# A two-layer hybrid encoder on one core: modulation as products and sums on VectorE, paced by TensorE's time

## The chip, the cores and the metric

The kernel runs on one core of a Trainium2 chip. Its time is the device time of one execution in microseconds (us); three runs of the kernel before gave 2958.4, 2958.51 and 2960.57 us, median 2958.51. The execution that the profiler recorded took 2961.13 us, of which 2959.30 us is the span from the first to the last recorded instruction. In this text a slot is one 128x1024 piece of streamed weights (512 KB), the unit in which the whole program is written; a tile of the modulation has the same size.

## The reference

Two layers, 256 tokens, width 2048, all in f32. Each layer turns the conditioning vector c into six vectors of 2048 (shift, scale and gate for two sub-layers), and then runs a token mixer and a gated convolutional MLP, both behind an RMS norm that scale and shift modulate:

```python
c_act = silu(c)                                   # (1, 2048)
for l in range(2):
    mod = c_act @ w_ada[l] + b_ada[l]             # (1, 6 * 2048)
    sh1, sc1, g1, sh2, sc2, g2 = split(mod, 6)
    h = rms_norm(x, g_norm1[l]) * (1 + sc1) + sh1
    x = x + g1 * hybrid_mixer(h, ...)             # attention, S5, pooling, three gates
    h = rms_norm(x, g_norm2[l]) * (1 + sc2) + sh2
    x = x + g2 * conv_ffn(h, ...)
```

The modulation is a product of a vector with a 2048 x 12288 matrix in each layer: 192 tiles of 512 KB a layer, 384 in all. The parts are numbered 0 to 5 in the order of the split. The S5 part of the mixer is a scan over time whose output y goes through a small projection (w_glu) and then through p_b into the merge of the branches.

## The kernel before, in words

All weights are streamed in 936 slots, 468 a layer. For every slot SyncE's queue fetches 512 KB (raw, four buffers), ScalarE rounds it to fp32r (whi, `make_hi`, four buffers), VectorE subtracts to get the rest (wlo, `make_lo`, three buffers), and TensorE multiplies: for each of the eight 128x128 blocks one pass of the high part with 512 columns (the high and low halves of the activation side by side) and one of the low part with 256 columns. `block_emitter` writes all eight high passes of a slot first (line 326), then all eight low ones (line 331). The low part of slot s+2 is written ahead of the products of slot s.

A layer's slots are, in this order and counted from the layer's first: the input projections (0 to 47), the gates and branch projections (48 to 177), w_out (178 to 209), and the MLP: up, down, up, down (210 to 467). `w_glu` stands at 160 and 161, behind twelve gate blocks.

Everything else is written by generators ("tasks") that `run_stream` steps once a slot. A task may run only while a credit is positive; every VectorE instruction takes its modelled time from the credit, and every slot gives 2.6 us. What a consumer needs at once is forced by `require`, whatever the credit. So the order of the instructions on each engine is fixed when the program is built, and a consumer that comes too early puts all of its producer's remaining instructions into the queues in one piece. The engines then run their queues in order, held by semaphores alone.

The modulation is a task of low rank, in groups of tiles (`ADA`), paced by a table of slot against tile (`ADA_PLAN`). 192 of its 384 tiles go to TensorE: c is spread over 32 columns and four 32-column strips of the array work side by side, two tiles and four products at a time. The other 192 go to VectorE, as two `scalar_tensor_tensor` of 128x512 each that accumulate into `acc`; eight tiles make one `acc`, which TensorE transposes in four pieces and VectorE reduces to four columns of `mod`. The norm of a sub-layer (`norm`, `hrhs`) turns x into the operand h two blocks at a time on VectorE and ScalarE, as soon as their entries of `mod` are there, and looks ahead by four blocks where it can:

```python
while o.n < min(k + 4, KT):
    ks = (o.n, o.n + 1)
    keys = [("mod", o.l, p, i) for p in (o.sh, o.sc) for i in ks]
    if o.n > k and any(key not in self.done for key in keys):
        break
```

Names in the rows: adaw is a modulation tile, cact the activated c, prod, tb, yt and yh are S5's, th the gates' tanh, mh the merged branches split in high and low, nt and h the norm's, x the residual, sqa the norm's sum of squares. Matmuls with f32 operands (modulation, S5, attention) stand as two records each.

## Time and profile before

| | |
|---|---|
| median of three runs | 2958.51 us |
| profiled execution | 2961.13 us, span 2959.30 us |
| TensorE busy | 2871.8 us, 97% of the span |
| VectorE busy | 2316.7 us, 78% |
| ScalarE busy | 1385.9 us, 47% |
| HBM traffic | 238 GB/s over the span |

A row of a timeline has start and length in us, the engine, the line of the kernel, the operation, what it writes and reads, and the count of the instructions merged into it; a bracket says how long the engine sat idle ahead of it and what it waited for. PE is TensorE, DVE VectorE, ACT ScalarE, POOL GpSimd. A busy TensorE is not TensorE at its peak: what a stretch costs is read from the start of one piece of work to the start of the next.

### The profile page before, as it was taken

How to read it: one execution, taken by the hardware profiler on the slowest of the kernel's cores; microseconds unless marked ns; L12 is line 12 of the kernel's file. 1: busy time of each engine (PE TensorE's matmuls, PEld its weight loads, DVE VectorE, ACT ScalarE, POOL GpSimd, SP SyncE). 2: the span in 40 equal slices, each digit the busy share in tenths (PEclk: the TensorE clock that was granted, in tenths of full speed). 3: DMA queues.
4: the chain of work that ended last, by engine and by line, in shares of the span. 5: the costliest groups of instructions: out<-in, count | busy, mean ns of one | idle time of the engine just before them, and what ended most of it. 6: DMA issues, size and time to landing. Idle time of an engine off the chain costs nothing.

```text
span 2959.3 us, 45094 instructions
## 1 busy us (share of the span) xinstructions
PE 2871.8 (97%) x16880; PEld 2431.4 (82%) x16880; DVE 2316.7 (78%) x4222; ACT 1385.9 (47%) x2209; POOL 43.6 (1%) x74
## 2 busy tenths in 40 slices
PE   6999999979999999999989999999999999999998
PEld 3787787758788888888868788888888888888887
DVE  5888677766698899999966887899888887556664
ACT  3355544434455543455434455555445554345542
POOL 0000000000000000000000000000000000000000
PEclk9999999989999999999999999999999999999999
DMA  9967767747677778888885555576676776555554
GB/s 368 351 221 254 239 235 259 247 144 277 207 257 252 254 274 295 294 283 302 299 300 198 197 180 181 192 244 239 246 267 207 241 236 204 187 191 187 189 193 151
DMA packets 195387, 705.97 MB, mean 239 GB/s; under 512 B 22496, under 2 KB 23008, under 8 KB 195168
## 3 DMA queue, kind: packets, MB, share of 16 engines
q1 hardware_dynamic: 190656, 691.23, 68.1%
q0 software_dynamic: 3648, 11.01, 1.0%
q8 instruction: 132, 2.16, 0.3%
q10 hardware_dynamic: 864, 0.86, 0.1%
q14 instruction: 87, 0.71, 0.1%
HBM read 698.82 MB, written 4.19 MB: 238 GB/s over the span
## 4 chain that ended last, share of the span: by engine, by line
PE 86%; issue 7%; DVE 5%; DMA 1%; ACT 0%; POOL 0%; POOLq 0%; SPq 0%; DVEq 0%; ACTq 0%
PE b L326 45%; PE b L331 23%; PE b L179 11%; PE b L355 6%; DVE wlo L154 2%; DMA adaw<-in_w_ada 1%; DVE acc L158 1%; PE b L569 0%; DVE prod L154 0%; DVE x L158 0%; POOL out L1497 0%; PE b L913 0%; DVE th L158 0%; DVE ftmp L154 0%; DVE m L154 0%
## 5 line engine op out<-in xcount | busy, mean ns | idle before, releaser
L154 DVE TENSOR_TENSOR wlo<-raw,whi 128x1024 fp32r<-128x1024 f32 x936 | 1136.9, 1215 | 509.9 <-PE b L331 252.8
L174 ACT ACTIVATE whi<-raw 128x1024 fp32r<-128x1024 f32 x936 | 980.8, 1052 | 914.3 <-PE b L326 443.7
L326 PE MATMUL b<-h,whi 128*128 128x512 f32 x4352 | 1104.5, 396 | 4.3 <-DVE h L158 4.3
L326 PEld LDWEIGHTS b<-h,whi 128*128 128x128 f32 x4352 | 784.6, 189 | 178.0 <-issue 18.7
L331 PEld LDWEIGHTS b<-h,wlo 128*128 128x128 f32 x4352 | 594.8, 191 | 43.7 <-DVE wlo L154 0.7
L331 PE MATMUL b<-h,wlo 128*128 128x256 f32 x4352 | 607.6, 282 | 0.3 <-DVE wlo L154 0.3
L326 PE MATMUL b<-hid,whi 128*128 128x512 f32 x1376 | 345.8, 393 | 3.2 <-DVE hid L158 3.2
L326 PEld LDWEIGHTS b<-hid,whi 128*128 128x128 f32 x1376 | 247.4, 189 | 49.1 <-DVE hid L158 4.1
L158 DVE SCALAR_TENSOR_TENSOR acc<-adaw,cact,acc 128x512 f32<-128x512 f32 x360 | 269.3, 748 | 5.2
L331 PEld LDWEIGHTS b<-hid,wlo 128*128 128x128 f32 x1376 | 187.6, 190 | 14.0 <-DVE wlo L154 0.7
L331 PE MATMUL b<-hid,wlo 128*128 128x256 f32 x1376 | 192.0, 282 | 0.3 <-DVE wlo L154 0.3
L179 PE MATMUL b<-whi,h 128*128 128x512 f32 (+1 forms) x512 | 155.2, 376 | 0.0
L326 PE MATMUL b<-mh,whi 128*128 128x512 f32 x512 | 130.7, 397 | 4.1 <-DVE mh L154 4.1
L174 ACT ACTIVATE fth<-ft 128x256 f32<-128x256 f32 x86 | 36.0, 418 | 199.1 <-DVE ft L158 199.1
L179 PE MATMUL b<-adaw,cact 128*32 128x512 f32 (+1 forms) x832 | 111.1, 582 | 9.0 <-DMA adaw<-in_w_ada 9.0
L179 PEld LDWEIGHTS b<-whi,h 128*128 128x128 f32 x512 | 94.1, 188 | 27.9 <-issue 9.5
L326 PEld LDWEIGHTS b<-mh,whi 128*128 128x128 f32 x512 | 92.6, 190 | 26.9 <-ACT whi L174 3.4
L179 PE MATMUL b<-wlo,h 128*128 128x512 f32 (+1 forms) x256 | 95.0, 371 | 0.0
L355 PE MATMUL b<-h,whi 128*128 128x256 f32 x384 | 78.1, 299 | 10.5 <-ACT whi L174 5.5
L174 ACT ACTIVATE hid<-ft 128x256 fp32r<-128x256 f32 x86 | 35.9, 418 | 108.9 <-DVE ft L154 108.9
L158 DVE SCALAR_TENSOR_TENSOR ft<-fa,lvecs,ft 128x255 f32<-128x255 f32 (+1 forms) x172 | 82.5, 481 | 3.0
L355 PEld LDWEIGHTS b<-h,whi 128*128 128x128 f32 x384 | 65.4, 205 | 15.7 <-ACT whi L174 6.6
(262 smaller groups left out, 2548.8 us busy)
## 6 DMA issues: line engine op xcount, KB each, us to landing
adaw<-in_w_ada SPq DMA_DIRECT2D x384, 512.0 KB, 5.5
raw<-in_w_up SPq DMA_DIRECT2D x344, 512.0 KB, 3.7
raw<-in_w_gate SPq DMA_DIRECT2D x192, 512.0 KB, 3.9
raw<-in_w_down_a SPq DMA_DIRECT2D x88, 512.0 KB, 3.5
raw<-in_w_down_b SPq DMA_DIRECT2D x84, 512.0 KB, 3.7
raw<-in_w_out SPq DMA_DIRECT2D x64, 512.0 KB, 4.4
raw<-in_w_q SPq DMA_DIRECT2D x32, 512.0 KB, 3.8
raw<-in_p_a SPq DMA_DIRECT2D x32, 512.0 KB, 4.4
```

What stands on the lines that cost most here:

```text
L154: self.nc.vector.tensor_tensor(out, a, b, op=op)
L158: self.nc.vector.scalar_tensor_tensor(out, a, s, b, op0=op0, op1=op1)
L174: self.nc.scalar.activation(out, a, func, bias=bias, scale=scale)
L179: self.nc.tensor.matmul(out, lhsT, rhs, start=start, stop=stop)
L326: self.nc.tensor.matmul(u.ps, hi[:, j * 128:(j + 1) * 128], x, start=u.cnt == 0, stop=False, skip_group_check=True)
L331: self.nc.tensor.matmul(u.ps[:, T:], lo[:, j * 128:(j + 1) * 128], x[:, :T], start=False, stop=last, skip_group_check=True)
L355: self.nc.tensor.matmul(ps, w, r, start=first and i == 0 and not u.after, stop=last and i == 2 and not u.before, skip_group_check=shared)
```

## The change

1. The credit is earned with every TensorE instruction (`earn`), by its modelled time, instead of 2.6 us a slot, and the modelled VectorE times are larger. Low tasks are stepped behind the others, and `require` steps its producer one piece at a time.
2. 248 of the 384 modulation tiles go to VectorE, in another layout: 128 output columns on the partitions, 1024 inputs along the row. One `tensor_tensor_reduce` multiplies such a tile by c (spread over all partitions, `crow`) and adds up the row into one column of `mod`; each column takes two, one for each half of c. There are no transposes and no reductions behind it. c's rows are made once at the start (16 products on TensorE, four copies, one write of 1 MB to DRAM) and a half of them is loaded whenever the half changes.
3. The 136 tiles that stay on TensorE go, from the 64th on, in steps of one tile (four products of 256 columns).
4. High and low passes come in turns: high, low for one slot, low, high for the next.
5. `w_glu` moves behind fourteen gate blocks, p_b is one piece behind all sixteen, layer 1's gates and projections are in layer 0's order, w_out runs over k for its first four units, and x is loaded again at its sixth slot.

```diff
-ADA_PLAN = ((0, 18), (8, 34), (18, 50), (30, 66), (48, 66), (140, 128), (204, 160), (296, 192), (460, 296), (580, 320), (670, 356), (770, 384))
+ADA_PLAN = ((0, 18), (8, 34), (18, 50), (30, 66), (48, 66), (154, 136), (180, 138), (200, 160), (240, 165), (462, 316), (490, 330), (630, 338),
+            (650, 340), (676, 352), (765, 384))
...
-        self.credit -= 0.069 + 1.04e-3 * self.size(out)
+        self.credit -= 0.155 + 1.04e-3 * self.size(out)
...
+    def mm(self, out, lhsT, rhs, start=True, stop=True, share=1, **kw):
+        n = self.size(rhs)
+        self.earn((n + 32) / 2400 if rhs.dtype == F32R else n / 600 / share)
+        self.nc.tensor.matmul(out, lhsT, rhs, start=start, stop=stop, **kw)
...
-            self.credit = max(min(self.credit + 2.6 * o.w / SLOT, 2.0), -2.0)
+            self.credit = max(min(self.credit, 2.0), -2.0)
...
+            for i, high in enumerate((True, False) if self.high_first else (False, True)):
+                for u, j, x, cnt in todo:
+                    out, w, r = (u.ps, hi, x) if high else (u.ps[:, T:], lo, x[:, :T])
...
+    def ada_sums(self, i0, l, tiles, first, ahead, last):
+        i = i0
+        for h in (first, 1 - first):
+            self.ada_on_pe = False
+            if self.crow_half != h:
+                self.crow = self.cpool.tile([128, 1024], F32, name="crow", tag="crow", bufs=1)
+                self.nc.gpsimd.dma_start(self.crow, self.c_rows[:, h * 1024:(h + 1) * 1024])
+                self.crow_half = h
+                for _ in range(4):
+                    yield None
+            for part, t in tiles:
+                self.ada_fetch(min(i + ahead, last))
+                w = self.ada_tiles.pop(i)
+                n = 16 * part + t
+                col = self.mod[l][:, n:n + 1]
+                seed = self.vec(l, "b_ada")[:, n:n + 1] if h == first else col
+                self.credit -= 0.16 + 1.04e-3 * 1024
+                self.nc.vector.tensor_tensor_reduce(w, w, self.crow, 1.0, seed, OP.mult, OP.add, col)
+                if h != first:
+                    self.done.add(("mod", l, part, t))
+                i += 1
+                yield 1
+                while self.ada_early(i):
+                    yield None
...
-        gates(1, every[:12])
+        gates(1, every[:14])
...
-        self.slots[n + 1].pre = load_x
+        self.slots[n + 5].pre = load_x
...
-        o = [(n, k) for ks in (range(12), range(12, KT)) for n in range(4) for k in ks]
+        o = [(n, k) for k in range(KT) for n in range(4)]
```

Where instructions stand now. First TensorE at the end of layer 0's last down-projection (hid is its operand, adaw the modulation of layer 1). Before:

```order
L331 MATMUL b_15218<-hid,wlo 128x256 x2
L179 MATMUL b_15232<-adaw,cact 32x512 x20
L326 MATMUL b_15218<-hid,whi 128x512 x8
L331 MATMUL b_15218<-hid,wlo 128x256 x8
L326 MATMUL b_15218<-hid,whi 128x512 x8
```

After:

```order
L191 MATMUL b_15077<-hid,whi 128x512 x14
L191 MATMUL b_15133<-hid,whi 128x512 x2
L191 MATMUL b_15077<-hid,wlo 128x256 x6
L191 MATMUL b_15133<-hid,wlo 128x256 x10
L191 MATMUL b_15133<-hid,whi 128x512 x16
```

The twenty products on ten modulation tiles are gone from TensorE's queue, and the passes of two neighbouring slots stand together, sixteen high or sixteen low in a row.

Second, VectorE at the beginning of layer 0's MLP, where the norm makes h for the up-projection: the last two pieces of h, with the low part of a slot ahead of each. Before:

```order
L154 TENSOR_TENSOR wlo<-raw,whi 128x1024
L158 SCALAR_TENSOR_TENSOR gsc<-mod_87,vecs 128x2
L158 SCALAR_TENSOR_TENSOR nt<-x,gsc,rs 128x256 x2
L158 SCALAR_TENSOR_TENSOR h<-nt,mod_87,h 128x256 x2
L154 TENSOR_TENSOR wlo<-raw,whi 128x1024
L158 SCALAR_TENSOR_TENSOR gsc<-mod_87,vecs 128x2
L158 SCALAR_TENSOR_TENSOR nt<-x,gsc,rs 128x256 x2
L158 SCALAR_TENSOR_TENSOR h<-nt,mod_87,h 128x256 x2
```

After, the last piece of h alone (each tensor_tensor_reduce is two rows, the product and the read of its sum):

```order
L163 TENSOR_TENSOR wlo<-raw,whi 128x1024
L598 ISA adaw,mod_88<-adaw,crow,mod_88 128x1024
L598 ISA mod_88 128x1
L598 ISA adaw,mod_88<-adaw,crow,mod_88 128x1024
L598 ISA mod_88 128x1
L598 ISA adaw,mod_88<-adaw,crow,mod_88 128x1024
L598 ISA mod_88 128x1
L598 ISA adaw,mod_88<-adaw,crow,mod_88 128x1024
L598 ISA mod_88 128x1
L167 SCALAR_TENSOR_TENSOR gsc<-mod_88,vecs 128x2
L167 SCALAR_TENSOR_TENSOR nt<-x,gsc,rs 128x256 x2
L167 SCALAR_TENSOR_TENSOR h<-nt,mod_88,h 128x256 x2
```

Four modulation tiles now stand ahead of this piece, two more ahead of the piece before it, and one ahead of that, each behind the wlo of a slot; both pieces have also moved two places later in the row of slots.

Third, VectorE at layer 1's `w_glu`, which needs S5's last output. Before:

```order
L154 TENSOR_TENSOR wlo<-raw,whi 128x1024
L154 TENSOR_TENSOR th_20446<-th_20446,b_20542 128x256
L158 SCALAR_TENSOR_TENSOR yt<-u,lvecs,b_19639 128x256
L165 TENSOR_SCALAR yt<-yt 128x256
L154 TENSOR_TENSOR yt<-yt 128x256
L158 SCALAR_TENSOR_TENSOR u<-yt 128x256
L154 TENSOR_TENSOR yh<-u,yh 128x256 x4
```

After, the last twelve of eighteen rows between a wlo and the next:

```order
L163 TENSOR_TENSOR prod<-b_20455,tb 128x512 x2
L163 TENSOR_TENSOR th_20450<-th_20450,b_20432 128x256
L163 TENSOR_TENSOR prod<-prod 128x256 x2
L1145 SCALAR_TENSOR_TENSOR prod<-r,prod 128x256 x2
L167 SCALAR_TENSOR_TENSOR prod<-prod,tb 128x256
L163 TENSOR_TENSOR prod<-prod,tb 128x256
L163 TENSOR_TENSOR prod<-prod,tb 128x2x256
L167 SCALAR_TENSOR_TENSOR yt<-u,lvecs,b_20041 128x256
L174 TENSOR_SCALAR yt<-yt 128x256
L163 TENSOR_TENSOR yt<-yt 128x256
L167 SCALAR_TENSOR_TENSOR u<-yt 128x256
L163 TENSOR_TENSOR yh<-u,yh 128x256 x4
```

Sixteen S5 products and scans (nine here, seven ahead of them) now stand in one piece ahead of yt, where before only the end of S5 stood. In layer 0 it is the other way: the piece ahead of yt held 25 such instructions and sixteen of the tables tb, and now holds twelve of the first kind and none of the second.

## Rows read from the trace of the kernel before

**Rows 1.** The page, part 1: busy us of each engine.
```profile
PE 2871.8 (97%) x16880; PEld 2431.4 (82%) x16880; DVE 2316.7 (78%) x4222; ACT 1385.9 (47%) x2209; POOL 43.6 (1%) x74
```
**Rows 2.** Timeline of PE, two undisturbed slots: start, length, engine, line, operation.
```profile
2415.81 2.00 PE L326 MATMUL b<-h,whi 128*128 128x512 f32 x8
2417.65 1.11 PE L331 MATMUL b<-h,wlo 128*128 128x256 f32 x8
2418.60 1.78 PE L326 MATMUL b<-h,whi 128*128 128x512 f32 x7
```
**Rows 3.** Stretches: us, busy PE, PEld, DVE, ACT, POOL, clock, DMA share, GB/s.
```profile
0.00:74.00 74.00, 46.62 (x312) 28.55 (x316) 37.99 (x149) 22.60 (x43) 2.14 (x7) 0.93 0.94 368
814.00:1554.00 740.00, 729.38 (x4183) 634.25 (x4181) 664.23 (x1098) 347.34 (x492) 8.64 (x16) 1.00 0.81 281
611.00:633.00 22.00, 9.29 (x38) 3.51 (x38) 13.92 (x39) 3.96 (x11) 0.00 (x0) 0.61 0.00 1
```
**Rows 4.** Timeline of PE at the end of layer 0.
```profile
1520.56 1.91 PE L179 MATMUL b<-adaw,cact 128*32 128x512 f32 x12
...
1525.38 1.05 PE L179 MATMUL b<-adaw,cact 128*32 128x512 f32 x4 [2.90 <-DMA adaw<-in_w_ada]
...
1536.59 2.11 PE L326 MATMUL b<-hid,whi 128*128 128x512 f32 x8
```
**Rows 5.** Timeline of PE: two modulation tiles, and eight in a row.
```profile
595.97 1.07 PE L179 MATMUL b<-adaw,cact 128*32 128x512 f32 x8
596.97 1.13 PE L179 MATMUL b<-u,bp 32*128 32x256 f32 x8
...
35.75 3.66 PE L179 MATMUL b<-adaw,cact 128*32 128x256 f32 x64
```
**Rows 6.** Timeline of PE: the transposes of one VectorE group.
```profile
1517.24 0.60 PE L569 MATMUL b<-const,acc 128*128 128x128 f32 x4
1517.60 2.09 PE L326 MATMUL b<-hid,whi 128*128 128x512 f32 x8
```
**Rows 7.** DVE by line and form: busy us, mean ns, idle before.
```profile
L154 DVE TENSOR_TENSOR wlo<-raw,whi 128x1024 fp32r<-128x1024 f32 x920 | 1123.8, 1222 | 498.9 <-PE b L331 252.8 <-issue 139.9 <-ACT fa L174 30.4
L158 DVE SCALAR_TENSOR_TENSOR acc<-adaw,cact,acc 128x512 f32<-128x512 f32 x360 | 269.3, 748 | 5.2
L1086 DVE TENSOR_TENSOR_SCAN prod<-r,prod 128x256 f32<-128x256 f32 x64 | 40.5, 675 | 0.0
```
**Rows 8.** Timeline of PE at layer 0's w_glu.
```profile
605.56 1.11 PE L331 MATMUL b<-h,wlo 128*128 128x256 f32 x8
...
623.47 1.06 PE L179 MATMUL b<-prod,cc 128*32 128x256 f32 x2 [7.43 <-DVE prod L154]
...
634.23 0.39 PE L355 MATMUL b<-yh,whi 128*128 128x256 f32 x1 [2.57 <-ACT yh L174]
```
**Rows 9.** Timeline of PE at layer 1's w_glu.
```profile
2065.81 1.91 PE L179 MATMUL b<-prod,cc 128*32 128x256 f32 x14 [0.60 <-DVE prod L154]
2070.29 0.39 PE L355 MATMUL b<-yh,whi 128*128 128x256 f32 x1 [2.57 <-ACT yh L174]
```
**Rows 10.** Timeline of PE at the first slots of w_out, layers 0 and 1.
```profile
696.78 0.47 PE L326 MATMUL b<-mh,whi 128*128 128x512 f32 x1 [1.65 <-DVE mh L154]
...
2125.99 1.66 PE L326 MATMUL b<-mh,whi 128*128 128x512 f32 x4 [2.46 <-DVE mh L154]
```
**Rows 11.** Timeline of DVE and PE, seventh and eighth slots of layer 0's MLP.
```profile
816.11 1.22 DVE L154 TENSOR_TENSOR wlo<-raw,whi 128x1024 fp32r<-128x1024 f32 x1
...
817.43 0.88 DVE L158 SCALAR_TENSOR_TENSOR nt<-x,gsc,rs 128x256 f32<-128x256 f32 x2
...
823.08 2.00 PE L326 MATMUL b<-h,whi 128*128 128x512 f32 x8
```
**Rows 12.** The chain that ended last, first 100 us.
```profile
53.68 9.30 DMA adaw<-in_w_ada
...
91.80 6.15 DMA adaw<-in_w_ada
```

More of the change, by code (lines that the diff above doesn't have):

```diff
@@ L195, in step_evacs, with step_task @@
         self.fresh = []
-    def step_task(self, t, force=False):
+    def step_task(self, t, force=False, once=False):
+        if once:
+            try:
+                next(t[0])
+            except StopIteration:
+                (self.tasks if t in self.tasks else self.low).remove(t)
+            return
         while force or (self.credit > 0 and self.acredit > -1.0):
@@ L208, in step @@
         self.step_evacs()
-        for t in list(self.low):
-            self.step_task(t, force=self.ada_on_pe)
+        low = list(self.low)
+        for t in low:
+            if self.ada_on_pe:
+                self.step_task(t, force=True)
         for t in list(self.tasks):
             self.step_task(t)
+        for t in low:
+            if t in self.low and not self.ada_on_pe:
+                self.step_task(t)
     def require(self, *keys):
@@ L354, in block @@
         for i, (w, r) in enumerate(ops):
-            self.nc.tensor.matmul(ps, w, r, start=first and i == 0 and not u.after,
-                                  stop=last and i == 2 and not u.before, skip_group_check=shared)
+            self.mm(ps, w, r, start=first and i == 0 and not u.after, stop=last and i == 2 and not u.before,
+                    skip_group_check=shared)
         if last:
@@ L493, in ada_fetch @@
             i = self.ada_next
-            pool, bufs = self.ada_ring if i < 64 and i % (NADA + APRE) < APRE else (self.cpool, NADA)
-            t = pool.tile([128, 1024], F32, name="adaw", tag="adaw", bufs=bufs)
+            r = i % (APRE + NADA + 1) if i < ADA_FIRST else APRE
+            if r == APRE + NADA:
+                t = self.cpool.tile([128, 1024], F32, name="adaw", tag="crow", bufs=1)
+            else:
+                pool, bufs = self.ada_ring if r < APRE else (self.cpool, NADA)
+                t = pool.tile([128, 1024], F32, name="adaw", tag="adaw", bufs=bufs)
             self.nc.sync.dma_start(t, self.a["w_ada"][i])
@@ new lines, in ada_group @@
+    def ada_group(self, i0, l, chunks, wt, ahead, last):
+        m = len(chunks)
+        self.ada_on_pe = True
+        b, ps = yield from self.take_bank()
+        i, n, width = i0, wt // 2, 128 * wt
+        for q in range(0, KT, 4 // m):
+            self.ada_fetch(min(i + n, last))
+            ws = [self.ada_tiles.pop(i + j) for j in range(n)]
+            for g in range(4):
+                k = q + g // m
+                cs = self.cact[:, k:k + 1].to_broadcast([128, 32])
+                w = ws[g * n // 4][:, g * width % 1024:][:, :width]
+                self.mm(ps[32 * g:32 * g + 32, :width], cs, w, start=q == 0, stop=q + 4 // m == KT, share=4)
+            i += n
+            self.ada_fetch(min(i + ahead, last))
+            while self.ada_early(i):
+                yield None
+            yield 1
@@ L580, in ada_task @@
         i = sum(2 * wt * len(chunks) for _, chunks, wt, _ in ADA[:lo])
-        for l, chunks, wt, on_pe in ADA[lo:hi]:
-            yield from self.ada_group(i, l, chunks, wt, on_pe, ahead, last)
+        for l, chunks, wt, first in ADA[lo:hi]:
+            if first is None:
+                yield from self.ada_group(i, l, chunks, wt, ahead, last)
+            else:
+                yield from self.ada_sums(i, l, chunks, first, ahead, last)
             i += 2 * wt * len(chunks)
@@ L1333, in layer @@
         oa = src("oa", ("oa", l, 0), ("oa", l, 1))
-        if l == 0:
-            gates(0, every[:8])
+        gates(0, every[:8])
         proj(2, "p_c", 4, src("oc", ("oc", l)), every)
-        if l == 0:
-            proj(0, "p_a", 8, oa, every[:8])
-        for g in range(0 if l else 4, 8):
+        proj(0, "p_a", 8, oa, every[:8])
+        for g in range(4, 8):
             ns = every[2 * g:2 * g + 2]
```

185 lines of the change are left out of this document (85 added, 100 removed).

## The prediction, made before the kernel was run

> **What bounds the kernel now.** I read the shares of the page first: TensorE is busy 97% of the span, VectorE 78%, ScalarE 47% [rows 1]. Then the timeline of TensorE where nothing disturbs it: a slot takes 2.79 us from high pass to high pass, of which the eight high passes take 1.84 and the eight low ones 0.95 [rows 2]. 936 slots of 2.79 us would be 2611 us, so some 350 us lie in other TensorE work and in waits, and these are what a change can win. The third view is the busy time by stretches: in the MLP of layer 0 TensorE runs 729 of 740 us while VectorE is busy 664 of them [rows 3], so VectorE is no bound there but has only a tenth to spare. Last, the timelines at the places where TensorE is idle or does modulation: the end of layer 0 [rows 4], S5 ahead of w_glu [rows 8, 9], the first slots of w_out [rows 10], the first 100 us, where the chain of waits goes through DMA [rows 12]. What leaves TensorE's queue counts in full; what moves on VectorE counts only where TensorE then waits.
>
> **The change part by part.** The sum is made against the profiled execution, 2961.13 us (span 2959.30 and 1.8 around it), which lies 2.6 us above the median.
>
> *Modulation of layer 1 off TensorE.* At the end of layer 0 twenty products on ten tiles hold TensorE from 1520.56 to 1536.59, 16.0 us, most of it waiting for tiles [rows 4]. Nothing stands in their place. The other 22 tiles of that group lie in layer 1's mixer, in eleven visits to TensorE of two tiles, 1.00 us each [rows 5], after which the next high passes take about 0.1 us more (2.09 to 2.11 us against 2.00) [rows 2, 4, 6]. 16.0 + 11 x 1.1 = 28.1 us gained.
>
> *Modulation of layer 0.* 96 tiles in 45 visits become 72 tiles in 60 visits. Eight tiles in a row take 3.66 us, 0.46 each, so a visit of two tiles has 0.08 us of its own, and 0.1 behind it [rows 5, 6]. 96 x 0.46 + 45 x 0.18 = 52.3, and 72 x 0.46 + 60 x 0.18 = 43.9: 8.4 us gained. (The first 64 tiles stand as before.)
>
> *Transposes.* 24 VectorE groups go, each with four transposes that keep TensorE 0.36 us and slow the next passes by 0.09 [rows 6]: 10.8 us gained. The sixteen products that spread c stand at the very start, when TensorE has nothing else.
>
> *The products on VectorE.* The trace has no tensor_tensor_reduce. From below it costs what wlo does, as many elements from two sources, 1.22 us, and nothing for the read of its sum; from above what the scan does, 0.675 us for 256 elements, so 2.70 [rows 7]. The rows nearest to it are wlo and the accumulating form, which has a column as operand too and takes 0.748 for 512, 1.50 for as many elements [rows 7]; I take halfway, 1.35 us, of which about 0.08 lies under the next instruction, as with wlo. In the stretch of 740 us 132 tiles as two 0.75 and sixteen reductions of about 0.7 come to 209 us; 141 new products at 1.27 are 179. VectorE would have 664 - 209 + 179 = 634 us to do in 716 (740 less 24 of TensorE work gone): no bound. So this part costs nothing where it is spread out, and up to about 1.7 us each it would stay so.
>
> The row of the accumulating form shows two f32 sources from SBUF at full rate, 0.748 us for 512 elements [rows 7]; it keeps no running sum. [...]
>
> *Seven products where TensorE waits for them.* At the start of layer 0's MLP the last two pieces of h are late in the order: one product, then two, then four stand in front of them. Before, the third-last low part began at 816.11 and the seventh slot's pace was kept; the eighth slot started at 823.08 [rows 11]. Now: low part until 817.3, next one until about 818.6, one product to 819.9, low part to 821.0, two products to 823.6, and the piece of h 1.7 us on: the seventh slot starts some 5 us late. Behind it a low part, four products (5.1 us) and the last piece: about 833.5, against 823.08. With two more for the clock, which fell to half in comparable waits, I take 13 us lost (nothing if VectorE runs further ahead than I think; 17 if the tiles come late as well, since a tile fetched three products earlier must have landed). In layer 1 two products stand so: 3 us lost. One more stands ahead of the norm at the turn of the layers: 1 us.
>
> *S5 ahead of w_glu.* One chain of nine products and scans takes 4.57 us (623.47 to 628.04 is one round, 0.51 each) [rows 8], and the end from the last products to yh 4.48 us at full clock (2065.81 to 2070.29) [rows 9]. Before, layer 0 lost 605.56 + 1.0 to 634.23, 27.7 us, less some 5 us of S5's own matmuls, and in the middle of it the clock was granted at 0.61 [rows 3, 8]: 24 us with the slow restart. Now twelve products, a low part and a gate's addition stand in that piece: 12 x 0.51 + 4.5 + 1.5 = 12 us, less two sets of matmuls (3.8 us), plus 2 to 3 of slow clock: 11 lost, so 13 gained. In layer 1 before, 2064.6 to 2070.29 less 1.9 of matmuls: 4 lost. Now sixteen products: 16 x 0.51 + 4.5 + 1.5 = 14, which begins 1 us before TensorE runs dry, less 3.8, plus 2 to 3: 12 lost, so 8 more than before.
>
> *w_out by k.* A slot now needs two blocks of mh instead of eight, so the waits of 1.65 and 2.46 us [rows 10] go, and about 1.5 us of half clock behind the second: 5.5 gained. What is late next is x: it is loaded four slots later and needed after the eighth slot, 3 slots or 8.4 us on; VectorE would wait for it, and TensorE has two slots of wlo in hand.
>
> *High and low in turns.* Seven high passes take 1.78 us as against 2.00 for eight, 0.22 each, and eight take 1.84 to the first low one [rows 2]: the change of kind costs under 0.04 us, so at half as many changes the gain is at most 0.02 x 812 slots, 16 us, and I take nothing. It has a price: every second slot needs its low part 1.84 us earlier. I take nothing here too, since VectorE sits idle 253 us waiting for a free wlo buffer, which is time in which it is ahead [rows 7]; the bound is the third rival.
>
> *Start.* In the first 74 us 368 GB/s are moved and the chain waits 9.3 and 6.2 us for tiles [rows 3, 12]; c's rows add 1 MB there: 1 / 0.368 = 2.8, 3 us lost. The queue of POOL gets the crow loads; each is followed by four slots (11 us) before it is used.
>
> *Sum.* -28.1 - 8.4 - 10.8 + 13 + 3 + 1 - 13 + 8 - 5.5 + 3 = -37.8. 2961.1 - 37.8 = 2923.3 for a profiled execution, 2920.7 against the median.
>
> **The rivals.** *Half rate.* If the product with its sum runs at half of wlo's rate, 2 x 1.22 less one start, about 2.3 us (1 us more than I take), VectorE has 664 - 209 + 141 x 2.25 = 772 us of work in a stretch of 716: TensorE waits for wlo at least 56 us, and nearer to 75, since the pieces of down cannot lend their spare time to up. The other 107 products add some 15, the ones in front of h another 9. That is about 80 to 99 us lost, say 95: 3016. It decides from 1.7 us a product, where VectorE fills the stretch. For it: the scan, which also carries a value from element to element, at 2.6 ns an element; against it: the accumulating form's full rate [rows 7]. [...]
>
> *The waits are covered.* If VectorE, now given work by TensorE's real time, is far enough ahead when S5's end and the norm's last pieces come, the 13 and 3 at the MLPs and the 8 in layer 1 go: 2920.7 - 24 = 2897. For it: the 253 us in which it waited for a buffer; against it: h and yh are forced, so the pieces stand in the queue as one and their length does not depend on what came before.
>
> *Turns cost.* With VectorE at 89% in the MLPs, every second slot's wlo has 1.84 us less. If half of the some 250 slots of the full stretches are low-first and each waits a quarter of a us, 125 x 0.25 = 31 us are lost: 2952. For it: the thin margin of that stretch; against: TensorE's 11 idle us in it so far [rows 3].
>
> *It does not do what it says.* The credit by TensorE's time could leave S5 as late as before: 13 us less gain, 2934, still on the same side.
>
> **How the numbers follow.** My forecast has 0.53, the covered waits 0.15, the turns' cost 0.17, half rate 0.10, S5 as late as before 0.05. The predicted time is 2921. Its own terms are uncertain by 10 to 15 us (S5 by 6 to each side, the norm's pieces from 0 to 17, the start from 0 to 4). The range goes from 2893 (the covered waits and a little of the turns' 16 us) to 2959 (the turns' cost with bad luck); half rate and the tails stay outside. A measurement of this kernel tells about 0.2%, 5.9 us, from no change: faster is under 2952.6, slower over 2964.4. Faster: 0.53 + 0.15 + 0.05 and half of the turns, 0.81; within: most of the other half, 0.08; slower: half rate and a remainder, 0.11.
>
> **What would show it.** No adaw on TensorE after the first third, and the last down slots of layer 0 at 2.79 us without a pause; tensor_tensor_reduce near 1.3 us; VectorE below 90% in layer 0's MLP and no wlo in TensorE's waits there; two gaps of 5 us at the seventh and eighth slot of layer 0's MLP; about 12 us without slots at each w_glu; no wait for mh in w_out. I am wrong if a product takes over 1.7 us, if the pieces ahead of h cost nothing, or if low-first slots wait for wlo again and again.

## The result and the profile after

The changed kernel takes 2982.9 us (median of six runs, 2976.66 to 2985.41), the kernel before 2959.14 in six runs on the same chip: ratio 1.0074 with a 95% interval of 1.0062 to 1.0087. It is 0.74% slower where 1.3% faster was forecast. The profiled execution took 2981.78 us, its span is 2980.0.

Part 1 of the page, the answer to [rows 1]:

```profile
PE 2852.0 (96%) x16874; PEld 2438.3 (82%) x16874; DVE 2323.0 (78%) x4292; ACT 1396.5 (47%) x2214; POOL 49.9 (2%) x84
```

TensorE is busy for 20 us less than before and the span is 21 us longer, so it stands idle for 40 us more. VectorE has hardly more work; it is not the bound. VectorE's groups by line (count, busy us, mean ns, idle before), answering [rows 7]:

```profile
L163 DVE TENSOR_TENSOR wlo<-raw,whi 128x1024 fp32r<-128x1024 f32 x936 | 1132.2, 1213 | 449.5 <-issue 223.2 <-PE b L191 180.6 <-ACT whi L183 23.8
L598 DVE CUSTOM_DVE_ANT_0 adaw<-adaw,crow,vecs 128x1024 f32<-128x1024 f32 x124 | 157.9, 1279 | 17.7 <-DMA adaw<-in_w_ada 17.4
L598 DVE CUSTOM_DVE_ANT_0 adaw<-adaw,crow,mod 128x1024 f32<-128x1024 f32 x124 | 157.8, 1279 | 26.7 <-DMA adaw<-in_w_ada 26.5
```

The product with its sum is the CUSTOM row: 1.279 us for 1024 elements, where 1.35 was taken. Half rate, some 2.3 us as the prediction worked it out from the 1.22 us of wlo, does not show: where two products follow each other the second starts 1.20 us after the first. What does show is 43.9 us in which products waited for their tile.

Where the time went, by stages. A stage runs from TensorE's first pass of its first slot to that of the next stage's first slot, in the two profiled executions (the first begins and the last ends with the span); the forecast's terms are put where they belong. The expectations below put 17.8 us on layer 1's w_glu and 11.6 on layer 0's; counted by passes they are 16.1 and 13.7.

```
slots (of 936)                     forecast   measured, us
0-47     input projections, start     +3        -0.5
48-147   layer 0: gates, attention    -8       +25.3
148-177  layer 0: w_glu, p_b         -13       -13.7
178-197  layer 0: w_out begins        -3        -1.6
198-221  w_out's end, norm, MLP      +13       +22.7
222-425  layer 0: MLP                 -8        -7.1
426-479  turn of the layers          -15       -11.4
480-623  layer 1: mixer              -14       -12.9
624-633  layer 1: w_glu               +8       +16.1
634-689  layer 1: w_out, norm          0        +7.6
690-935  layer 1: MLP                 -1        -3.8
sum                                  -38       +20.7
```

The steady parts came out. Five places did not: layer 0's mixer (33 us off), the start of its MLP (10), layer 1's w_glu (8), its w_out with the norm (8), and the turn of the layers (4). All five are places where TensorE has to wait for something that VectorE or a tile's fetch brings late.

*Start of layer 0's MLP*, timeline of DVE, PE and SP's queue, answering [rows 11]:

```profile
829.14 1.28 DVE L598 CUSTOM_DVE_ANT_0 adaw<-adaw,crow,mod 128x1024 f32<-128x1024 f32 x1
829.62 1.16 SPq L538 DMA_DIRECT2D adaw<-in_w_ada  x2
...
833.09 1.28 DVE L598 CUSTOM_DVE_ANT_0 adaw<-adaw,crow,mod 128x1024 f32<-128x1024 f32 x1 [2.66 <-DMA adaw<-in_w_ada]
...
836.09 3.78 PE L191 MATMUL b<-h,whi 128*128 128x512 f32 x8 [7.72 <-DVE h L167]
...
847.80 1.28 DVE L598 CUSTOM_DVE_ANT_0 adaw<-adaw,crow,mod 128x1024 f32<-128x1024 f32 x1 [2.65 <-DMA adaw<-in_w_ada]
...
852.43 2.08 PE L191 MATMUL b<-h,wlo 128*128 128x256 f32 x8 [10.95 <-ACT h L183]
```

Seven products stand here as predicted (one, two, four), and TensorE stops twice. But the later ones of a group wait for their tiles (2.7 us the second of two, 2.7 and 0.9 the third and the fourth of four): there are three buffers, and a fetch is queued only behind the product that frees its buffer. And eight high passes behind the first stop take 3.78 us instead of 2.00 as in [rows 2]. The stretch (PE busy, clock, DMA share, GB/s) shows why:

```profile
820.00:870.00 50.00, 31.33 (x148) 0.76 0.54 183
```

The granted clock averages 0.76: it is 0.50 from 831.0 to 841.2 us and again from 844.7 to 858.3, from within each stop into the passes behind it, and 1.00 elsewhere in the stretch.

*Layer 0's mixer*, timeline of PE, answering [rows 5]:

```profile
305.15 1.50 PE L191 MATMUL b<-adaw,cact 128*32 128x256 f32 x24
309.62 1.08 PE L191 MATMUL b<-adaw,cact 128*32 128x256 f32 x8 [2.96 <-DMA adaw<-in_w_ada]
...
312.51 5.27 PE L191 MATMUL b<-h,whi 128*128 128x512 f32 x16
```

A new group of tiles catches up with four tiles in a row, on three buffers; the fourth is not there for 3 us, and sixteen high passes then take 5.27 us instead of 3.82 (those that begin at 300.46). The same wait, 3.11 us, stands behind the tiles at 407.55.

*Layer 1's w_glu*, timeline of DVE and PE, answering [rows 9]:

```profile
2070.39 0.23 DVE L167 SCALAR_TENSOR_TENSOR tb<-tb,nsn,pr 128x16 f32<-128x16 f32 x1 [3.68 <-ACT pr L183]
2070.54 0.23 DVE L167 SCALAR_TENSOR_TENSOR tb<-tb,sn,pr 128x16 f32<-128x16 f32 x1
...
2076.63 1.28 DVE L598 CUSTOM_DVE_ANT_0 adaw<-adaw,crow,vecs 128x1024 f32<-128x1024 f32 x1
...
2086.35 1.06 PE L191 MATMUL b<-prod,cc 128*32 128x256 f32 x2 [6.60 <-DVE prod L163]
...
2097.04 0.39 PE L191 MATMUL b<-yh,whi 128*128 128x256 f32 x1 [2.56 <-ACT yh L183]
```

S5 still makes its tables here, with six of its 32 scans to come behind slot 624 (two before the change). The first two rows matter below: one starts 0.15 us after the other, though each is recorded with 0.23.

*Turn of the layers*, timeline of DVE and PE, and the stretch behind, answering [rows 4]:

```profile
1543.98 1.28 DVE L598 CUSTOM_DVE_ANT_0 adaw<-adaw,crow,vecs 128x1024 f32<-128x1024 f32 x1 [3.30 <-DMA adaw<-in_w_ada]
1546.47 1.21 PE L191 MATMUL b<-hid,wlo 128*128 128x256 f32 x8 [2.38 <-DVE wlo L163]
...
1564.83 0.95 PE L685 MATMUL b<-const,sqa 128*128 128x1 f32 x4 [2.58 <-DVE sqa L163]
1568.44 1.01 PE L685 MATMUL b<-const,sq 128*128 128x1 f32 x4 [2.66 <-ACT sq L183]
```

```profile
1565.00:1580.00 15.00, 9.76 (x48) 0.55 0.39 121
```

The 16 us of modulation on TensorE are gone, but second products in a row now hold up wlo and the sum of squares, and the norm runs at a clock of 0.55. While TensorE held the modulation before the change, VectorE could catch up just ahead of the norm; that this cover is what was lost is argued, not shown.

### The profile page after: what moved, and what is told of

It reads as the page before. It is cut to its first block, busy times and chain, and to the rows that moved or that the text cites. A ratio compares the mean times of both kernels' runs of the same rounds, so it can differ in the third digit from the quotient of the medians.

```text
span 2980.0 us, 45155 instructions
## 1 busy us (share of the span) xinstructions
PE 2852.0 (96%) x16874; PEld 2438.3 (82%) x16874; DVE 2323.0 (78%) x4292; ACT 1396.5 (47%) x2214; POOL 49.9 (2%) x84
## 4 chain that ended last, share of the span: by engine, by line
PE 84%; DVE 6%; issue 5%; DMA 4%; ACT 1%; POOL 0%; SPq 0%; ACTq 0%; POOLq 0%; DVEq 0%
PE b L191 84%; DMA adaw<-in_w_ada 3%; DVE wlo L163 2%; DVE adaw L598 1%; PE b L195 0%; DVE prod L163 0%; DVE m L163 0%; DMA raw<-in_w_qi 0%; DVE th L167 0%; DMA raw<-in_w_q 0%; POOL out L1552 0%; DMA posi<-in_pos 0%; DVE tb L167 0%; DVE x L167 0%; ACT pr L183 0%
## 5 line engine op out<-in xcount | busy, mean ns | idle before, releaser
L191 PE MATMUL b<-h,whi 128*128 128x512 f32 (+1 forms) x4736 | 1140.1, 387 | 24.1 <-DVE h L167 16.8
L191 PEld LDWEIGHTS b<-h,whi 128*128 128x128 f32 x4736 | 869.8, 191 | 194.8 <-issue 15.6
L191 PE MATMUL b<-h,wlo 128*128 128x256 f32 x4544 | 640.8, 286 | 18.2 <-ACT h L183 14.7
L191 PE MATMUL b<-hid,whi 128*128 128x512 f32 x1376 | 331.0, 392 | 2.7 <-DVE hid L167 2.7
L191 PE MATMUL b<-hid,wlo 128*128 128x256 f32 x1376 | 178.7, 283 | 2.4 <-DVE wlo L163 2.4
L598 DVE CUSTOM_DVE_ANT_0 adaw<-adaw,crow,mod 128x1024 f32<-128x1024 f32 x124 | 157.8, 1279 | 26.7 <-DMA adaw<-in_w_ada 26.5
L598 DVE CUSTOM_DVE_ANT_0 adaw<-adaw,crow,vecs 128x1024 f32<-128x1024 f32 x124 | 157.9, 1279 | 17.7 <-DMA adaw<-in_w_ada 17.4
L191 PE MATMUL b<-adaw,cact 128*32 128x256 f32 (+1 forms) x896 | 81.4, 438 | 11.0 <-DMA adaw<-in_w_ada 11.0
L167 DVE SCALAR_TENSOR_TENSOR tb<-tb,nsn,pr 128x16 f32<-128x16 f32 (+3 forms) x128 | 35.4, 277 | 55.3 <-ACT pr L183 55.0
L191 PEld LDWEIGHTS b<-mh,wlo 128*128 128x128 f32 x512 | 66.4, 192 | 3.3 <-ACT mh L183 0.5
```

Of the source, the lines that this page charges most:

```text
L167: self.nc.vector.scalar_tensor_tensor(out, a, s, b, op0=op0, op1=op1)
L191: self.nc.tensor.matmul(out, lhsT, rhs, start=start, stop=stop, **kw)
L598: self.nc.vector.tensor_tensor_reduce(w, w, self.crow, 1.0, seed, OP.mult, OP.add, col)
```

## The experiments

All medians are of 4 to 11 runs; a ratio is to the kernel before, run on the same chip, with its 95% interval. Differences between two runs are of their medians, and the kernel before took 2959.1 to 2962.0 us beside them, so they are uncertain by up to 3 us. Lines left out of a cut are marked "...".

### The credit

**Old credit.** The changed kernel with the credit of before:

```diff
...
-        self.credit -= (0.155 if isinstance(s, float) else 0.215) + 1.04e-3 * self.size(out)
+        self.credit -= (0.069 if isinstance(s, float) else 0.13) + 1.04e-3 * self.size(out)
...
-        self.credit += us
...
-            self.credit = max(min(self.credit, 2.0), -2.0)
...
+            self.credit = max(min(self.credit + 2.6 * o.w / SLOT, 2.0), -2.0)
...
-                    self.credit -= 1.35
+                    self.credit -= 0.68
```

> The changed kernel with the credit of before: 2.6 us a slot and the smaller modelled VectorE times, all else as changed. Theory: with the larger modelled times S5 is given fewer pieces a slot, and so it comes to w_glu late in layer 1 (17.8 us more than before) though VectorE has idle time in the mixer; with the old credit layer 1's loss goes to 0 to 5 us, and layer 0, where the four gate blocks in front of w_glu help in any case, keeps most of its 11.6: 2968 us. Rival: the credit is what brought layer 0's gain and the products and the order make layer 1's loss: layer 0 loses its 12, layer 1 keeps its 18, and the time is 2990 us or more.

2947.2 us, 0.9958 [0.9946, 0.997]: 36 us better than the changed kernel, more than the theory said. No scan is left behind slot 624 of layer 1, and w_glu follows the gates' passes at once (timeline of PE):

```profile
2083.83 2.00 PE L191 MATMUL b<-h,whi 128*128 128x512 f32 x8
2085.67 0.28 PE L191 MATMUL b<-yh,whi 128*128 128x256 f32 x1
```

Stage by stage against the changed kernel: layer 1's w_glu 23 us better, its w_out with the norm 15, slots 148 to 177 of layer 0 10, the start of its MLP 17; worse in layer 0's MLP by 24 (slots 302 to 345 alone 18), where VectorE is overdrawn and TensorE waits for wlo (the profiled execution took 2954.02 us, 7 over the median, so the stages add up to 28 us and not 36):

```profile
1107.45 1.21 PE L191 MATMUL b<-hid,wlo 128*128 128x256 f32 x8 [0.58 <-DVE wlo L163]
...
1120.45 1.21 PE L191 MATMUL b<-hid,wlo 128*128 128x256 f32 x8 [1.62 <-DVE wlo L163]
```

**New credit in the kernel before**, and nothing else.

> The kernel before with the new credit alone: earned by TensorE's modelled time, with the larger modelled VectorE times; its modulation, order of gates, turns and steps stay. Theory: this is the part that cost the changed kernel its time; S5 comes late to both w_glu (some 20 us in layer 1 and some 5 more in layer 0) and the split of mh with it: 2959 + 25 = 2984 us. Rival: the credit hurts only together with the products, which take VectorE's time in the mixers; alone it is worth 5 us at most to either side: 2954 to 2964 us.

2989.54 us, 1.0096 [1.0082, 1.011]: 29 us lost by the credit alone; the theory's total holds, its places only in part. Ten scans are left behind slot 624 in layer 1, and between 2061.01 and 2099.32 TensorE stands still for 26 of 38 us (timeline of PE):

```profile
2061.01 1.13 PE L182 MATMUL b<-u,bp 32*128 32x256 f32 x8
2072.48 1.06 PE L182 MATMUL b<-prod,cc 128*32 128x256 f32 x2 [10.33 <-DVE prod L154]
...
2088.97 1.06 PE L182 MATMUL b<-prod,cc 128*32 128x256 f32 x2 [6.29 <-DVE prod L154]
...
2099.32 0.39 PE L182 MATMUL b<-yh,whi 128*128 128x256 f32 x1 [2.56 <-ACT yh L174]
```

Layer 1 lost 37 us there, where the theory had 20, and 21 more in its mixer. In layer 0 slots 148 to 177 came 13 us better, where the theory had 5 lost, and slots 80 to 95 lost 12.

**Old modelled times only** (the credit still earned by TensorE's time).

> The changed kernel with the modelled VectorE times of before, but the credit still earned by TensorE's time: half of the credit's change undone, to see which half cost the 36 us that the old credit gave back. Theory: the larger modelled times are it. They count every instruction with its full duration, though the trace shows the next one starting about 0.07 us before the last one ends, so VectorE is given some 15% less small work than it could do. Then this kernel is like the one with the old credit in the mixers (2 to 5 us better, since a slot earns 2.77 instead of 2.6) and worse in the MLPs, where VectorE is overdrawn a little more: 2940 to 2955 us. Rival: the fixed 2.6 us a slot is it, and the modelled times matter little: 2975 to 2990 us.

2963.51 us, 1.0008 [0.9999, 1.0017]: 19 us of the 36. Layer 1's w_glu is 22.6 us better, exactly as with the whole old credit. So the modelled times matter, and the rival falls, but the theory's range is missed by 8 us: small times and generous earning together are worse than the old credit by 14 us in layer 0's slots 64 to 111 and by 23 in layer 1's 504 to 575, probably overdrawing VectorE there as both do in the MLP.

**Credit by stage**: old up to each MLP's twelfth slot, new behind it.

```diff
...
+    def mixer(self):
+        return self.slot_no % 10000 % 468 < 222
...
```

> The changed kernel with the credit of before in the mixers, up to the twelfth slot of each MLP, and the new credit in the rest of the MLPs. Theory: the old credit helps where TensorE waits for a task (S5, mh, the norm's tiles) and hurts where nothing is waited for but wlo: in the MLP of layer 0 the kernel with the old credit lost 24 us more than the changed one to waits for wlo, while it won 60 in the other stages. So 2947 - 24 = 2923 us, without waits over 1 us for wlo between 860 and 1430 us. Rival: the products that the MLP does not get done on time are then late at the end of layer 0 or have to be done in layer 1's mixer: 2935 to 2947 us.

2941.63 us, 0.9927 [0.9913, 0.9941]. Layer 0's MLP gave the 24 us, but slots 634 to 665 of layer 1 took 12 back: the products that the MLP no longer does stand there and ahead of w_glu, 27 in slots 620 to 665 instead of 9. The rival's time came.

### Tiles and products

**Norm's tiles on TensorE**:

```diff
-ADA += [(0, [(4, 8), (3, 8)], 2, None)]
-ADA += [(0, [(p, t) for t in range(10, 16) for p in (4, 3)], 1, 0)]
+ADA += [(0, [(p, 8 + j) for j in (0, 4) for p in (4, 3)], 4, None)]
```

> The changed kernel with all tiles of layer 0's parts 3 and 4 (shift and scale of the MLP's norm) on TensorE, 24 more than in the changed kernel, in groups of four columns, so that no product stands on VectorE ahead of h. Theory: the 22.7 us that w_out's end and the first slots of the MLP lost are these products, the wait of 2.7 us for their tiles and the half clock behind each stop. They go, S5 loses its few products too, and TensorE gets 24 x 0.46 us and eight more visits of 0.18, 12.5 us, part of it in time in which it waits for S5: 2983 - 23 + 10 = 2970 us. Rival: the stop is x or the norm itself, later because w_out goes by k and x is loaded four slots later; then the stops at the seventh and eighth slot stay and the time is 2993 us.

2973.78 us, 1.0044 [1.0032, 1.0056]: 9 us better, 13 forecast. Both stops are gone (slots 198 to 221 take 1.6 us less than before the change), so all of the 22.7 us were the products; 14 us of TensorE work stand in slots 178 to 197 instead.

**Fourth buffer** for the tiles on TensorE in layer 0's mixer:

```diff
...
+                r = APRE + (i % (NADA + 1) if i < 136 else 0)
...
```

c's row, which is not there yet, lends its place.

> The changed kernel with a fourth buffer for modulation tiles 64 to 135, the ones that TensorE works on in layer 0's mixer (c's row, which is not there yet, lends its place). Theory: the two stops of about 3 us, each where a new group starts and catches up with four tiles in a row, come from the fourth tile, whose fetch can only start when the first is used; with them go two stretches of 6.8 us at half clock, 3 to 3.5 us each: 13 us less, 2970 us, and no stop over 1 us there. Rival: the catching up itself costs the time, or the fetch queue is late whatever the buffers: 2980 to 2986 us with the stops in place.

2974.14 us, 1.0042 [1.003, 1.0054]: 9 us, and no tile on TensorE waits there any more; slots 48 to 147 are 13 us better.

**Cap**: at most two TensorE steps and one product in a slot.

> The changed kernel with at most two steps of TensorE's modulation and one product of VectorE's in a slot (after the first 48 slots, and not where a consumer forces them), so that nothing catches up in a burst. Theory: what stops TensorE in layer 0's mixer is a burst of four to eight tiles after a group had to wait for a free bank, and what delays the norm at the turn of the layers is two products in a row on VectorE, the second of which waits 2.7 to 3 us for a tile whose fetch could start only behind the first: both need more tiles than there are buffers. Capped, the mixer wins the 9 us that the fourth buffer won, the turn of the layers some 5 (its two waits of 2.5 and 2.7 us and part of 13.7 us of half clock): 2969 us. Rival: the products and tiles then fall behind the plan and are forced at the norm and at x's load: 2985 us or more.

3077.8 us, 1.0394 [1.038, 1.0409]: the theory's cure failed, the rival was right by far more than it said. One product a slot is not enough to keep the plan, some 50 products are forced ahead of layer 1's norm, and slots 634 to 689 take 127 us more than in the changed kernel. The run prices a forced product (SP's queue, then PE, then DVE):

```profile
2276.88 41.44 SPq L539 DMA_DIRECT2D adaw<-in_w_ada  x20
```

```profile
2321.97 3.35 PE L192 MATMUL b<-h,whi 128*128 128x512 f32 x7 [44.31 <-DVE h L168]
```

```profile
2314.26 1.28 DVE L603 CUSTOM_DVE_ANT_0 adaw<-adaw,crow,mod 128x1024 f32<-128x1024 f32 x1 [7.12 <-DMA crow<-c_rows]
```

Twenty fetches take 41.44 us, 2.07 each, with no other fetch on SP's queue: a run of products is paced by its tiles on three buffers (ahead of the row's change they begin 2.0 us apart, 14 steps from 2277.56 to 2305.85), and where the half of c changes, a product waits 7.12 us for its row. With the slow passes behind the stop (seven high passes take 3.35 us, against 1.78 in [rows 2]) it is 127 / 48 = 2.6 us for each of the 48 more than in the changed kernel. The cap does not tell what bursts alone cost.

The same cap on the faster version below (credit by stage, norm's tiles on TensorE, fourth buffer) was expected to bring it to 2914 us, its rival 2929 or more. It took 2992.43 us, 1.0105 [1.0091, 1.0119], 64 us more than without the cap: 32 products are forced ahead of layer 1's norm.

### The edit of w_out

**Old order and early x**:

```diff
...
-        o = [(n, k) for k in range(KT) for n in range(4)]
+        o = [(n, k) for ks in (range(12), range(12, KT)) for n in range(4) for k in ks]
...
-        self.slots[n + 5].pre = load_x
+        self.slots[n + 1].pre = load_x
...
```

> The changed kernel with w_out's order of before (four blocks over twelve k, then over the last four) and x loaded at its second slot again. Theory: the new order was worth nothing, since the waits for mh stayed (3.3 and 2.1 us in layer 0, 2.1 us in layer 1, against 1.8 and 2.6 before): mh is late as a whole under the new credit, and with eight blocks asked for in the first slot more of the wait moves to the front: 2983 to 2990 us. Rival: the new order did save its 5.5 us or more, and other things ate it: 2990 us or more, with a wait of over 5 us at w_out in each layer. Or the late load of x is a loss: under 2980 us.

2959.44 us, 0.9996 [0.9987, 1.0005]: 23 us better, the last case named. **Early x alone** tells the halves apart:

> The changed kernel with x loaded at w_out's second slot as before, and w_out in its new order by k: half of the edit that won 23 us. Theory: the late load of x is what cost them, since the modulation's part 2 and x come later, the additions to x are put off, and products with them; then 2962 us or so, with one stop instead of two at the start of layer 0's MLP. Rival: the order by k is what cost them (mh is asked for in sixteen small forced pieces, and each is taken from the credit): 2980 to 2985 us.

2966.07 us, 1.0016 [1.0007, 1.0025]: 17 of the 23 us are the place of the load, the other 6.6 the order by k. With the early load 20 products instead of 17 are done ahead of the norm, 4 instead of 7 are forced, and one of the two stops goes (timeline of PE):

```profile
825.20 1.11 PE L191 MATMUL b<-h,wlo 128*128 128x256 f32 x8
837.22 2.08 PE L191 MATMUL b<-h,wlo 128*128 128x256 f32 x8 [10.91 <-ACT h L183]
```

Three products more in slots 178 to 189 are counted. Why there is argued only: the early load forces all that is left of mh in one piece, and the credit is clipped at -2 us a slot, so the debt is forgiven; the late load leaves mh to be paid for slot by slot.

### Turns and the gates' order

**No turns** in the changed kernel, and **turns alone** in the kernel before (the cut is the first run's edit):

```diff
-            if todo:
-                self.high_first = not self.high_first
```

> The changed kernel with all eight high passes first in every slot, as before the change. Theory: the turns save TensorE about 0.013 us a slot (its steps of high passes fell from 230.6 to 228.5 ns between the two traces), some 10 us over 812 slots, and cost nothing: 2993 us, the slot in a steady stretch of the MLP back at 2.795 us. Rival: the turns are themselves a loss, since every second slot needs its low part 1.84 us sooner and VectorE is late in front of h and S5: 2970 us or less, with shorter stops at the start of layer 0's MLP.

> The kernel before with the turns alone: the high and the low passes change places in every second slot, as in the changed kernel, and nothing else. Theory: the turns save about 0.013 us a slot where nothing waits, and in the changed kernel their removal cost 11 us in all; here, where VectorE is further ahead, 8 to 11 us faster: 2950 us. Rival: they are worth only the 3 us that the two MLPs showed, and the rest of the 11 was waits of the changed kernel that moved: 2956 to 2960 us.

2994.62 us, 1.0114 [1.0101, 1.0127], and 2950.2 us, 0.9962 [0.9948, 0.9975]: 12 us and 11 us from both sides. Both theories hold.

**w_glu behind twelve gates.**

> The changed kernel with w_glu at its old place, behind twelve gate blocks instead of fourteen; the other gates follow it. Theory: S5 is on VectorE's path and the four slots, 11.1 us, are time it gains; with w_glu earlier TensorE waits 11 us longer in each layer and the clock falls for longer: 2983 + 22 + 2 = 3007 us, the waits at w_glu 11 us longer in both layers. Rival: S5's pieces are forced in one go and take their time wherever w_glu stands, the slots in front of it give them no credit to spare: less than 8 us lost, 2991 us at most.

2990.36 us, 1.0091 [1.0076, 1.0105]: 7 us by the medians, but the interval overlaps with the changed kernel's, so a loss is not shown. The theory's 24 us did not come, and the rival's "less than 8" holds. Six scans are left behind slot 624, as in the changed kernel.

### A faster version

**Together**: credit by stage, norm's tiles on TensorE, fourth buffer.

> All that helped, together: the credit by stage, the tiles of the MLP's norm on TensorE, and a fourth buffer for TensorE's tiles of layer 0. Theory: the three losses are separate places, so they add up: from the credit by stage (2923 us if its theory holds) 9 us for the buffers and 5 for the norm's tiles (16 us of stop are left there under the old credit, 9 us of TensorE work come in): 2908 us. Rival: they share the same room (with the old credit the tiles are forced earlier or later, and the stops move elsewhere): no better than the credit by stage alone, 2920 us or more.

2928.86 us, 0.9888 [0.9874, 0.9902]: 13 us better than the credit by stage alone, the theory's sum missed by 21, as that credit's own did by 19. In its mixer a burst of eight tiles is left, after 43 us without any, which I put down to a group that waits for a free bank (timeline of PE):

```profile
333.22 1.93 PE L197 MATMUL b<-adaw,cact 128*32 128x256 f32 x32
337.14 0.64 PE L197 MATMUL b<-adaw,cact 128*32 128x256 f32 x8 [1.98 <-DMA adaw<-in_w_ada]
...
341.04 1.08 PE L197 MATMUL b<-adaw,cact 128*32 128x256 f32 x8 [1.97 <-DMA adaw<-in_w_ada]
```

**Wider groups** there (32 tiles, four columns):

> The kernel with all that helped together, and the tiles 64 to 127 of layer 0 in groups of 32 tiles and four columns, two tiles a step, as before the change, instead of groups of 16 tiles and one tile a step. Theory: what is left of the loss in layer 0's mixer (19 us in slots 80 to 103) comes with the change of groups: a new group waits for a free bank while attention holds them, and then catches up with eight tiles in a row on four buffers. Half as many changes of group in the mixer: the burst at slot 86 goes or gets half as long, 8 to 15 us less, 2917 us. Rival: the loss there is not the groups (the credit of before in the mixer lets VectorE fall behind attention): 2926 to 2932 us with the loss in place.

2929.11 us, 0.9886 [0.9872, 0.9899]: no change. In the profiled executions (this run's lies 8 us under its median) the mixer, slots 48 to 147, won 19 us, and slots 148 to 177 lost 13. As I read it, S5 on VectorE ends last there, and a stop of TensorE ahead of it had been time for S5.

**No products at the turn**: the plan's `(240, 165), (462, 316)` becomes `(240, 165), (450, 316), (472, 316.5)`.

> The kernel with all that helped together, and no products between slots 452 and 472, the turn of the layers; they are done a little faster before it (0.72 a slot instead of 0.68). Theory: the stops at the turn (2.3 and 5.4 us, and half clock behind them) come from second products in a row that wait 3.05 us each for their tile, with wlo and the residual's additions behind them in VectorE's queue; without them the turn costs what it cost before apart from the modulation, 10 us less, 2919 us. Rival: the norm's own chain (sum of squares, rsqrt, h) stops TensorE there for 5 us anyway, which before the change followed right on modulation work; then 2925 to 2929 us.

2926.12 us, 0.9883 [0.9869, 0.9896]: 3 us by the medians, inside the noise, and not 10. As many products stand there as without it (11 in slots 455 to 467), so this does not settle the turn.

**Old w_out edit** in it:

> The kernel with all that helped together, and w_out's order and x's load as before the change. Theory: in the changed kernel the old order won 23 us because three more products got done ahead of the norm, and the norm's tiles are on TensorE here, so only the smaller part is left, 1 to 3 us at w_out in layer 1 and up to 5 at its norm: 2922 to 2927 us. Rival: the order itself is worth its 20 us, whatever stands ahead of the norm: 2912 us or less.

2935.49 us, 0.9914 [0.9901, 0.9928]: 7 us worse by the medians, with intervals that just touch; here, with the norm's tiles on TensorE, the order by k with the later load is probably the better one. **With the pause and the wider groups**:

> Everything that helped, with the pause at the turn of the layers and layer 0's tiles 64 to 127 in groups of 32. The wider groups took 15 us out of the mixer and gave 15 us back at w_glu, where S5 came late by as much, so they are not expected to add anything: the pause's 2926 us, or 2920 to 2929. Against the kernel before: 1.1 to 1.3% faster.

2924.38 us, 0.9873 [0.9859, 0.9886], the lowest median: 1.3% under before, 2% under the changed kernel, and as expected no clear gain over the pause alone.

## Why the prediction was wrong

Right: modulation off TensorE (layer 1's mixer -12.9 against -14), the transposes in layer 0's MLP (-7.1 against -8), VectorE no bound there, a product's 1.28 us, layer 0's w_glu (-13.7 against -13, as much as the new credit alone gives there), the start (-0.5 against +3). Neither half rate nor waiting low passes came.

*The step that failed first: "S5 ahead of w_glu", and with it all that the credit does.* I counted S5's left-over pieces at the two w_glu and took the new credit's effect from them. The credit sets the pace of all VectorE work, and I gave it no term of its own. It alone costs the kernel before 29 us, and taking it out gives the changed kernel 36. At layer 1's w_glu, where 8 us were forecast and 16.1 came, the larger modelled times are the cause: with the old ones 22.6 us come back. With larger charges S5 gets fewer pieces a slot, and comes late where TensorE needs it. They are larger in two ways. The new times are the recorded durations, but an instruction starts before the last one's record ends: the table step is charged 0.215 + 0.017 = 0.23 us and takes 0.15; the old charge was 0.13 + 0.017 = 0.147. And a pair of scans, charged 0.68 us before, is charged 1.35; it takes 1.29 from its start to the next one's (timeline of DVE of the changed kernel):

```profile
2088.42 1.26 DVE L1145 TENSOR_TENSOR_SCAN prod<-r,prod 128x256 f32<-128x256 f32 x2
2089.71 0.42 DVE L167 SCALAR_TENSOR_TENSOR prod<-prod,tb 128x256 f32<-128x256 f32 x1
```

So the old charges fit the small steps and were half of the truth for the scans. In a chain of nine, the two scans are charged 0.67 us more than before and the seven others 0.60 together (0.086 each). Every run with old times changes both, so which of the two made S5 late stays open. The earning by TensorE's time costs the rest of the 36 us: with the old times it takes 2963.51 us against 2947.2.

*"What is late next is x ... VectorE would wait for it, and TensorE has two slots of wlo in hand."* I costed the later load at nothing. It costs 17 us, 13 of them at the norm, where three more products stand in front of h.

*"w_out by k": 5.5 gained.* The waits for mh were to go. They grew, from 1.65 us to 5.6 in layer 0 and from 2.46 to 5.9 in layer 1, since mh is now waited for more than once (timeline of PE of the changed kernel):

```profile
704.38 3.53 PE L191 MATMUL b<-mh,whi 128*128 128x512 f32 x8 [3.17 <-DVE mh L163]
...
714.68 3.56 PE L191 MATMUL b<-mh,whi 128*128 128x512 f32 x8 [1.91 <-DVE mh L163]
```

With the early load the order by k is 7 us slower than the old one.

*"Seven products where TensorE waits for them": 13 us.* The count was right, the price was not: 22.7 us, all of it gone with the products. I bounded it by 17 "if the tiles come late as well" and took 13. They came late: the two stops are 18.7 us where my times gave some 10, and 6.2 us of that are products that waited for tiles. The low clock behind the stops took about 5 us, not the two I gave it: the passes from 836.09 to 841.48 and from 852.43 to 859.85 take 12.8 us, and 7.6 at the pace of the undisturbed slots.

*"Modulation of layer 0": 8.4 gained.* By place this is the largest miss: the mixer lost 25.3 us. I took the price of an evenly spaced visit. The visits come in bursts after each change of group, on one buffer less: 13 us by the fourth buffer's run. The rest is not settled. The old credit does not bring it back (slots 48 to 147 are 2 us slower with it); the wider groups do in the faster version, but there the time does not fall with it.

*"I take nothing" for the turns:* 11 us gained, inside the bound of 16. *End of layer 0:* 16 us of modulation went and 5 came back as stops of the norm and low clock; the products held back there did not leave the place, so how much they bear is open.

## What to carry to other kernels

A budget that paces one engine's work decides when each consumer's input is ready, so a change of it needs a term of its own in the forecast. A recorded duration was more than the distance from one start to the next, which is what the engine has to spend (0.23 us against 0.15 for a table step, 1.28 against 1.20 for a product); that charging this distance everywhere would be best is not shown, since the old charges, which did better, were too small for the scans. A budget by stage did better than either credit everywhere (2941.63 us against 2947.2 and 2982.9): strict where nothing but the stream waits, generous where a consumer waits for a task. Work that is forced in front of a consumer costs what its slowest supply takes, here 2 us a tile for a 1.28 us instruction, and 2.6 with c's row and the slow passes behind the stop. In a hand-ordered program even moving one load by four slots moves the background work; count what then stands ahead of each consumer.

## What the runs showed of the hardware

High and low passes in turns save 11 us. Two slots take 5.56 us from low pass to low pass (timeline of PE of the changed kernel), against 2 x 2.79 in [rows 2]; in the run with turns alone some 4 of the 11 us lie in the two MLPs and 6 in slots 198 to 221 and 426 to 479, and why they come there is not settled:

```profile
2404.38 2.08 PE L191 MATMUL b<-h,wlo 128*128 128x256 f32 x16
...
2409.94 2.08 PE L191 MATMUL b<-h,wlo 128*128 128x256 f32 x16
```

Product and sum over 1024 f32 elements of two SBUF operands took 1.279 us, with 0.08 for the read of the sum, the start of the next 1.20 us on. A run of 512 KB tile fetches on three buffers went at 2.07 us each, 253 GB/s, c's row within it, where the first 74 us of the kernel before move 368 [rows 3].
